# Two-layer hybrid encoder in split single precision: the forms of x for the feed-forward made in the attention's output projection, and pairs 3 to 21 by seven products

## The chip, the cores and the metric

The kernel runs on one core of one Trainium2 chip. The metric is the device time of one launch in microseconds. The core's engines are TensorE (PE: matmuls, with weight loads, PEld, beside them), VectorE (DVE), ScalarE (ACT), GpSimd (POOL, used here almost only to issue accumulating DMAs) and SyncE (SP, which issues the loads).

## What is computed

Two layers over x (512 rows of 1024) with a memory of 256 rows. Each layer has a mixer (attention of two kinds in layer 0, a chunked mLSTM in layer 1), a cross-attention to the memory and a gated feed-forward with a causal convolution of three taps. All in float32.

```python
for layer in range(DEPTH):
    xn = rms_norm(x, mix_norm[layer])
    ...
    x = x + mixed
    x = x + memory_cross_attention(rms_norm(x, xattn_norm[layer]), rms_norm(mem, mem_norm[layer]),
                                   xattn_wq[layer], xattn_wkv[layer], xattn_wo[layer])
    x = x + conv_ffn(rms_norm(x, ffn_norm[layer]), ffn_w_up[layer], ffn_conv_w[layer],
                     ffn_conv_b[layer], ffn_w_down[layer])
return rms_norm(x, final_norm)

def conv_ffn(xn, w_up, conv_w, conv_b, w_down):
    h = causal_depthwise_conv(xn @ w_up, conv_w) + conv_b
    g, u = jnp.split(h, 2, axis=-1)
    return (jax.nn.gelu(g) * u) @ w_down
```

w_up has 1024 x 5632 elements, w_down 2816 x 1024.

## The kernel before

**Numbers.** x lies in SBUF transposed: eight tiles `x[k]` of 128 features by 512 rows. Every float32 operand of a product is cut into two parts that TensorE takes at full rate: hi is a rounded copy (a cast on ACT), lo is the value less hi (`sub`, L265, on DVE; both together are `split`, L267). A product is three matmuls, hi by hi, hi by lo and lo by hi (`mm3`, L271, matmuls on lines 274 to 276). A weight block of 1024 columns comes by SP into one of three `raw` buffers and is split into `wh` and `wl` (three buffers each). So each block costs ACT a cast and DVE a subtraction before PE can use it.

**Cross-attention (`xattn`, L993).** Keys `kth`, `ktl` and values `vh`, `vl` of the memory are split tiles of 128 x 2048 in the stage's pool; the transposed weights of the softmax stand in `pth`, `ptl`; the heads' output rows in `mixed` (heads 0 and 1) and in the buffers `mem` (heads 2 and 3), which held the memory's own rows before. The stage ends with the output projection `p_out` (L375): eight output blocks m, each of eight k, each followed by the sum into x (`xadd`, L492) on DVE and by `xprep` (L478): x times the gain of the next norm on ACT with its split on DVE (`xh`, `xl`), and the sum of squares (`squares`, L461). The blocks run in the order 0 to 7. A planner (`Plan`) orders the tasks of this stage by costs written by hand.

**Feed-forward (`ffn_steps`, L1118).** The up projection has 44 blocks of 128 outputs in 22 pairs: block p (gate) and block 22 + p (value). Each pair ends in `tail` (L1246): convolution (the first tap on ACT, L1256, the other two on DVE, L1263), gelu on ACT, the product (L1273), and a split into `ah`, `al`, ten buffers each. The down projection is cut into five chunks of pairs (`CHUNKS`: four of four pairs, the last of six), each with eight output blocks, whose sums go to x by `xadd`. `fill` (L1424) puts down blocks of a finished chunk between the products of the later pairs from pair 5: three in a seven pair, two in a plain one. The queue gets eight blocks each at pairs 5, 9, 13 and 18; at pair 19 the last four in the queue are held back (`late`) until after pair 21. Then come the eight blocks of the last chunk (in layer 1 in `finish`, with the last norm and the output).

A pair is made in one of two ways.

`plain` (L1290): two blocks of 8 k x 3 matmuls of 512 columns, 48 matmuls, weights loaded by SP into `raw`.

`seven` (L1309): the two weight blocks, halved in the input features, and x, halved in features and in rows, form a 2 x 2 by 2 x 2 product in Winograd's form: seven products of 4 k x 3 matmuls of 256 columns, 84 matmuls. Three of them use x itself (`xh`, `xl`), four use the forms of x, T1 to T4, in `th` and `tl`. The weight side needs sums: `sa` is a load by SP with a second load added to it by POOL's DMA (`onto`, L1317), `sb` is made on DVE (L1340, then L1346), and five splits: f3 and f1 of 1024 columns, `s2`, `s4` and `a22` of 512. The results are put together by five operations of 256 columns on DVE (`sum_`, L1380: `u2`, `u3` and three quarters of `hs`) and two on ACT, and scaled by the norm (`scaled`, L1401). The tiles for `s2`, `s4`, `a22`, `ra`, `v`, `u2` and `u3` have one buffer each, `sb` and `dr` two, `sa` three.

```python
SEVEN = (4, 5, 6, 7, 8, 9, 10, 11, 12, 13, 14, 15, 17, 18, 19, 20)
p6 = pe(n, lambda: opened("Y", by, "acc", s2, 0, *T2, "Y", True), [w2, *formed], [("acc", by)], [("s2", s2)])
p5 = pe(n, lambda: opened("R", br, "s", f1, 512, *T1, "R", True), [w1], [("s", br)])
```

Pairs 0 to 3, 16 and 21 are plain. The forms are made by `forms(k)` (L1222) in the feed-forward, two of the four k after pair 0 and two after pair 1. For k it scales x[k] and x[k + 4] on ACT into an `hs` buffer, makes T1 and T3, T2, T4 on DVE in an `sa` buffer (512, 256 and 256 columns), casts the 1024 columns on ACT and subtracts on DVE. The sum of any down block into x waits on all forms, since they read x.

**Order.** `Sched` in the feed-forward is a list scheduler that runs when the program is built: each task has an engine, a cost and a due time written by hand, and buffers it takes and frees. It fixes the order in which each engine's instructions are issued; on the chip the engines wait on each other by semaphores. SP issues its loads in that order, and a load whose buffer is not free holds up those behind it.

Of the kernel before, what the change touches and what calls it, by code (L numbers as in the profile page):

```python
# [9 lines left out]
F32 = mybir.dt.float32  # L10
# [14 lines left out]

SEVEN = (4, 5, 6, 7, 8, 9, 10, 11, 12, 13, 14, 15, 17, 18, 19, 20)
EPS = 1e-6
# [192 lines left out]
class Builder:  # L220
# [153 lines left out]

    def p_out(self, pl, src, mixed, kdeps, gain, gi, order, prio, reload=False, order0=None):  # L375

        state = {}
        done = []
        for m in range(KB8):
            e = self.p_proj(  # L380
                pl, src[m], mixed, lambda ps, m=m: self.xadd(m, ps, reload), (("D", 0.6),), kdeps=kdeps, order=order, prio=prio + m
            )
            done.append(
                pl.add(lambda m=m: self.xprep(m, gain, gi, state), 0, [e], prio + m, chain=(("A", 0.52), ("D", 0.66), ("A", 0.52)), order=[order0])
            )
        self.state = state
        self.xdone = {k: [d] for k, d in enumerate(done)}

# [336 lines left out]
    def mix0(self):  # L725
        nc, t, tc = self.nc, self.t, self.tc
        with tc.tile_pool(name="mix0", bufs=1, reuse_waits="tile") as mp:
# [61 lines left out]
            def gates(ps):  # L789
                z = rows["z"] = self.til(self.memp, "mem", bufs=8)[:8, :]  # L790
# [135 lines left out]
    def p_memory(self, pl, layer, at, step, order=()):  # L926
# [16 lines left out]
        for k in range(KB8):  # L943

            def prep(k=k):
                both = self.til(mp, "mem", (P, 2, MEM), F32R, bufs=8)
# [46 lines left out]
    def xattn(self, layer):  # L993
        nc, t, tc = self.nc, self.t, self.tc
        with tc.tile_pool(name=f"xa{layer}", bufs=1, reuse_waits="tile") as mp:
            self.mp = mp
            pl = Plan(self.plan, [st["banks"][0] for st in self.fills], s=2, w=2, e=4, q=2, pt=2, wt=3)
            self.pad(mp, 192)
# [3 lines left out]
            vh = mp.tile([P, 2, DM], F32R, name=f"xvh{layer}")  # L1002
            vl = mp.tile([P, 2, DM], F32R, name=f"xvl{layer}")
            norm = self.x_norm(pl, 0, deps=self.xdone[7])
# [3 lines left out]
            for h in range(4):  # L1008
# [48 lines left out]

                def ptget(pts=pts):
                    pts["h"] = self.til(mp, "pth", (P, 2, 512), F32R)
                    pts["l"] = self.til(mp, "ptl", (P, 2, 512), F32R)  # L1060
# [34 lines left out]
                for d in range(2):  # L1095

                    def weigh(h=h, d=d, pts=pts):
# [4 lines left out]
                        b = 2 * h + d  # L1102
                        mh[b], ml[b] = (self.til(mp, "mixed", dtype=F32R, bufs=8) if h < 2 else self.til(self.memp, "mem", dtype=F32R, bufs=8) for _ in range(2))
                        self.split(mh[b][:], ml[b][:], ps[:])
# [13 lines left out]
    def ffn_steps(self, layer, mp):  # L1118
# [22 lines left out]
        RAWS = {"raw": (self.wp, 1024, 3), "dr": (mp, 512, 2), "sa": (mp, 1024, 3), "sb": (mp, 512, 2), "ra": (mp, 512, 1)}  # L1141

        def raw_tile(st, tag):
            pool, n, bufs = RAWS[tag]
            st[tag] = self.til(pool, tag, (P, n), bufs=bufs)
            return st[tag]
# [75 lines left out]
        def forms(k, at):  # L1222

            st = {}

            def scaled(j):
                if j == 0:
                    st["t"] = hs2[st["_hs"]][:, :, 2:514]
                nc.scalar.activation(st["t"][:, j, :512], self.x[k + 4 * j][:], AF.Identity, scale=self.col("ffn", layer * 8 + k + 4 * j))

            def first():
                st["r"] = raw_tile(st, "sa")[:]
                tt_(out=pair(st["r"][:, :512]), in0=pair(st["t"][:, 0, :512]), in1=st["t"][:, :, 256:512], op=ALU.subtract)

            T1, T3, T2, T4 = (slice(256 * i, 256 * i + 256) for i in range(4))
            tt_ = nc.vector.tensor_tensor
            a = add("ACT", ACV, lambda: scaled(0), (), at, [("hs", st)])
            a = add("ACT", ACV, lambda: scaled(1), [a], at)
            a = add("DVE", tt(512), first, [a], at, [("sa", st)])
            a = add("DVE", tt(256), lambda: tt_(out=st["r"][:, T2], in0=st["t"][:, 1, 256:512], in1=st["r"][:, T1], op=ALU.add), [a], at)  # L1240
            a = add("DVE", tt(256), lambda: tt_(out=st["r"][:, T4], in0=st["t"][:, 1, 0:256], in1=st["r"][:, T2], op=ALU.subtract), [a], at, (), [("hs", st)])
            h = add("ACT", act(1024), lambda: nc.scalar.copy(th[k][:], st["r"]), [a], at)
            formed.append(add("DVE", tt(1024), lambda: self.sub(tl[k][:], st["r"], th[k][:]), [h], at, (), [("sa", st)]))


        def tail(p, st, deps, at):  # L1246
# [27 lines left out]

            def hi():
                acts[p] = tuple(self.til(mp, n, dtype=F32R, bufs=10) for n in ("ah", "al"))
                nc.scalar.copy(acts[p][0][:], u())
# [31 lines left out]
        def seven(p, fill):  # L1309
# [16 lines left out]
            def small(s, tag):  # L1326
                if tag == "s4" and not pads:
                    pads.append(self.pad(mp, 64))
                s["wh"], s["wl"] = (self.til(mp, tag + i, (P, 512), F32R, bufs=1) for i in "hl")

# [37 lines left out]
            p1 = pe(n, lambda: opened("X", bx, "acc", f3, 0, *X(0, 0), "X", True), [w3], [("acc", bx)])  # L1368
            p6 = pe(n, lambda: opened("Y", by, "acc", s2, 0, *T2, "Y", True), [w2, *formed], [("acc", by)], [("s2", s2)])
            p5 = pe(n, lambda: opened("R", br, "s", f1, 512, *T1, "R", True), [w1], [("s", br)])  # L1370
            get = rows(st, at + 2.0)

            def v_():
                st["v_"] = self.til(mp, "v", (P, 256), bufs=1)
                nc.scalar.activation(st["v_"][:], st["X"][:, :256], AF.Copy, scale=-1.0)

            def sum_(tag, out, a, b, op):
                if tag:
                    st[tag] = self.til(mp, tag, (P, 256), bufs=1)
                tt_(out=out(), in0=a(), in1=b(), op=op)  # L1380

            bank = lambda n_: (lambda: st[n_][:, :256])
            tmp = lambda n_: (lambda: st[n_][:])
            hs = lambda j, l: (lambda: st["hs_"][:, j, 2 + 256 * l : 258 + 256 * l])
# [26 lines left out]
        def down(c, m, steps=1):  # L1411
# [227 lines left out]
    def finish(self, mp, ah, al):  # L1639
# [6 lines left out]
        HALF = [slice(0, 256), slice(256, 512)]  # L1646
        outs = [self.til(mp, f"t{i}{k}", (P, 1024), F32R, bufs=1).bitcast(F32)[:, s] for k in range(4) for i in "hl" for s in (slice(0, 512),)]

# [19 lines left out]
        def write(ps, t, f, r, vector):  # L1668
            out = outs.pop(0)
            if vector:  # L1670
                nc.vector.tensor_scalar(out=out[:], in0=ps[:], scalar1=r, scalar2=None, op0=ALU.mult)
            else:
                nc.scalar.activation(out[:], ps[:], AF.Identity, scale=r)
            (nc.sync if f else nc.scalar).dma_start(self.t["y"][t][:, f * 512 : f * 512 + 512], out[:])

# [32 lines left out]
    def run(self):  # L1708
        tc = self.tc
        M = bass.MemoryType.PSUM  # L1710
        with (
# [10 lines left out]
            for layer in range(2):  # L1722
                with tc.tile_pool(name=f"mem{layer}", bufs=1, reuse_waits="tile") as self.memp:
                    (self.mix0, self.mix1)[layer]()
                    self.xattn(layer)
                self.ffn(layer)

# [87 lines left out]
```

## Time and profile before

| | us |
|---|---|
| median of 3 runs | 1497.66 (1497.33 to 1498.31) |
| the profiled execution | 1497.39 |
| its span | 1495.6 |
| PE busy in the span | 1483.6 |
| DVE busy | 1194.5 |
| ACT busy | 806.0 |
| feed-forward of layer 0 | about 417 to 758 |
| feed-forward of layer 1, its last part excepted | about 1141 to 1481 |

A row of the timeline gives the start, the duration, engine, line and operation with out<-in. A matmul's duration overlaps with the next one's start, so PE's rate is read from start to start. On DVE too an instruction may start 0.08 us before the one ahead of it has ended by the profile. A row of windows gives for a stretch of time the busy time of each engine and, in brackets, its instructions, then the granted clock, the DMA engines' busy share and GB/s.

### The profile page before, as it was taken

The numbers are of one execution on the slowest core, as the hardware profiler recorded it, in microseconds if no ns is written. First come the engines' busy times: TensorE is split into PE (matmuls) and PEld (weight loads), VectorE is DVE, ScalarE is ACT, GpSimd is POOL, SyncE is SP. The second block draws the span as 40 slices with busy tenths as digits, with TensorE's granted clock in tenths as the row PEclk, the third lists the DMA queues.
The fourth block names the chain that finished last, engine by engine and source line by source line (L and its number), as shares of the span: only waits on it lengthen the run. The fifth ranks groups of instructions, "written<-read, shape, count | busy, mean of one in ns | idle before, by whom it ended". The sixth has DMA issues, their size and how long they took to land.

```text
span 1495.6 us, 22361 instructions
## 1 busy us (share of the span) xinstructions
PE 1483.6 (99%) x8426; PEld 1281.9 (86%) x8426; DVE 1194.5 (80%) x2255; ACT 806.0 (54%) x1349; POOL 57.8 (4%) x100
## 2 busy tenths in 40 slices
PE   9999999999999999999999999999999999999998
PEld 7888777888889999999888778888888899998987
DVE  7779795666589999989768857666567999999974
ACT  7777573444466455555446634444444655555544
POOL 0000130000001000000000000000000000000000
PEclk9999999999999999999999999999999999999999
DMA  5212223323237665542232222323323756564322
GB/s 195 85 63 79 85 86 115 125 74 125 85 127 192 168 157 154 148 120 89 75 99 85 71 99 84 99 93 120 113 72 126 183 156 169 149 162 134 94 65 76
DMA packets 60796, 171.76 MB, mean 115 GB/s; under 512 B 6672, under 2 KB 6672, under 8 KB 60688
## 3 DMA queue, kind: packets, MB, share of 16 engines
q1 hardware_dynamic: 55072, 152.43, 31.2%
q0 software_dynamic: 4608, 16.78, 6.6%
q8 instruction: 66, 1.08, 0.3%
q10 hardware_dynamic: 1008, 1.12, 0.2%
q14 instruction: 42, 0.34, 0.1%
HBM read 168.21 MB, written 2.10 MB: 114 GB/s over the span
## 4 chain that ended last, share of the span: by engine, by line
PE 93%; DVE 4%; ACT 2%; issue 1%; DMA 0%; SPq 0%; DVEq 0%; ACTq 0%
PE acc L274 19%; PE acc L276 19%; PE acc L275 19%; PE w L275 5%; PE w L274 5%; PE w L276 5%; PE s L274 3%; PE acc L335 2%; PE s L276 2%; PE acc L337 2%; PE acc L336 2%; PE s L275 2%; PE w L1603 1%; DVE wl L265 1%; PE s L401 1%
## 5 line engine op out<-in xcount | busy, mean ns | idle before, releaser
L274 PE MATMUL acc<-xh,wh 128*128 128x512 f32 (+1 forms) x832 | 301.3, 362 | 0.0
L276 PE MATMUL acc<-xh,wl 128*128 128x512 f32 (+1 forms) x832 | 296.8, 357 | 0.0
L275 PE MATMUL acc<-xl,wh 128*128 128x512 f32 (+1 forms) x832 | 296.6, 356 | 0.0
L265 DVE TENSOR_TENSOR wl<-raw,wh 128x1024 fp32r<-128x1024 f32 (+2 forms) x201 | 240.5, 1197 | 44.2 <-ACT wh L268 39.9
L268 ACT CAST wh<-raw 128x1024 fp32r<-128x1024 f32 (+2 forms) x137 | 140.6, 1029 | 164.7 <-PE acc L275 97.5
L275 PEld LDWEIGHTS acc<-xl,wh 128*128 128x128 f32 x832 | 157.2, 189 | 22.0
L276 PEld LDWEIGHTS acc<-xh,wl 128*128 128x128 f32 x832 | 156.2, 188 | 22.7
L274 PEld LDWEIGHTS acc<-xh,wh 128*128 128x128 f32 x832 | 156.3, 188 | 22.1
L1263 DVE SCALAR_TENSOR_TENSOR c<-hs,vec,c 128x512 f32<-128x512 f32 x176 | 128.8, 746 | 4.5 <-ACT c L1256 3.7
L275 PE MATMUL w<-al,wh 128*128 128x512 f32 x304 | 118.6, 390 | 0.0
L274 PE MATMUL w<-ah,wh 128*128 128x512 f32 x304 | 118.5, 390 | 0.0
L276 PE MATMUL w<-ah,wl 128*128 128x512 f32 x304 | 118.4, 389 | 0.0
L1256 ACT ACTIVATE c<-hs,vec 128x512 f32<-128x512 f32 x88 | 69.8, 813 | 52.9 <-DVE hs L1401 46.5
L276 PEld LDWEIGHTS w<-ah,wl 128*128 128x128 f32 x304 | 57.0, 188 | 12.0
L274 PEld LDWEIGHTS w<-ah,wh 128*128 128x128 f32 x304 | 57.1, 188 | 10.2
L275 PEld LDWEIGHTS w<-al,wh 128*128 128x128 f32 x304 | 57.1, 188 | 10.1
L495 DVE TENSOR_TENSOR x<-w,x 128x512 f32<-128x512 f32 x72 | 49.3, 685 | 16.1 <-PE w L276 16.1
L274 PE MATMUL acc<-mem,wh 128*128 128x256 f32 (+1 forms) x192 | 61.5, 320 | 0.0
L276 PE MATMUL acc<-mem,wl 128*128 128x256 f32 (+1 forms) x192 | 61.0, 318 | 0.0
L275 PE MATMUL acc<-mem,wh 128*128 128x256 f32 (+1 forms) x192 | 60.8, 317 | 0.0
L495 DVE TENSOR_TENSOR x<-acc,x 128x512 f32<-128x512 f32 x32 | 22.1, 690 | 46.6 <-PE acc L276 46.6
L1165 ACT CAST wh<-dr 128x512 fp32r<-128x512 f32 x64 | 39.5, 617 | 35.7 <-PE w L275 18.4
(373 smaller groups left out, 3798.2 us busy)
## 6 DMA issues: line engine op xcount, KB each, us to landing
raw<-in_up_dram SPq DMA_DIRECT2D x56, 512.0 KB, 3.3
dr<-in_down_dram SPq DMA_DIRECT2D x64, 256.0 KB, 2.9
sa<-in_up_dram SPq DMA_DIRECT2D x32, 512.0 KB, 3.5
sa<-in_up_dram POOLq DMA_DIRECT2D x32, 512.0 KB, 5.6
raw<-in_xk_dram SPq DMA_DIRECT2D x16, 512.0 KB, 3.2
raw<-in_wo_dram SPq DMA_DIRECT2D x16, 512.0 KB, 3.3
raw<-in_xq_dram SPq DMA_DIRECT2D x16, 512.0 KB, 3.2
raw<-in_xv_dram SPq DMA_DIRECT2D x16, 512.0 KB, 3.2
```

Of the source, the lines that this page charges most:

```text
L265: self.nc.vector.tensor_tensor(out=lo, in0=v, in1=hi.bitcast(F32), op=ALU.subtract)
L268: self.nc.scalar.copy(hi, v)
L274: mm(out, wh, xh, start=first, stop=False, skip_group_check=parts)
L275: mm(out, wh, xl, start=False, stop=False, skip_group_check=parts)
L276: mm(out, wl, xh, start=False, stop=last, skip_group_check=parts)
L335: mm(ps, xh[k][:, ts], wh[:, ws], start=(k == 0), stop=False)
L336: mm(ps, xh[k][:, ts], wl[:, ws], start=False, stop=False)
L337: mm(ps, xl[k][:, ts], wh[:, ws], start=False, stop=(k == 7))
L495: self.nc.vector.tensor_tensor(out=self.x[m][:], in0=ps[:], in1=self.x[m][:], op=ALU.add)
L1165: nc.scalar.copy(st["wh"][:, :cols], st[tag][:, :cols])
L1256: nc.scalar.activation(st["c_"][:, j, :], hs()[:, j, 2:514], AF.Identity, scale=self.col("cw", (layer * 3 + 2) * 44 + blk), bias=self.col( ...
L1263: nc.vector.scalar_tensor_tensor(out=c, in0=hs()[:, j, n : n + 512], scalar=w, in1=c, op0=ALU.mult, op1=ALU.add)
```

## The change

1. `SEVEN` becomes 3 to 21: pairs 3, 16 and 21 of each layer are made by seven products too. Six pairs more in all.
2. `forms` leaves the feed-forward. `p_forms` makes the same four groups in the output projection. The projection's blocks run in the order 0, 4, 1, 5, 2, 6, 3, 7, so that x[k] and x[k + 4] follow each other, and the forms of k come after block k + 4. Their scratch lies in the buffers `pth` and `ptl`.
3. The keys and values get tiles of their own, `kv0` to `kv3` (128 x 2048 each), in a pool that lives through cross-attention and feed-forward. `th` and `tl` are written into them when the attention is done with them; the feed-forward's own tiles for `th` and `tl` are gone.
4. Small tiles of the feed-forward move into buffers that lie idle there: `s2h`, `s2l`, `a22h`, `a22l`, `ra`, both `dr` and one `sb` into `mem0` to `mem7`; `v` into `memrb`, `u2` and `u3` into the two buffers of `sqt`. The number of buffers of each stays. `finish` writes its outputs from `kv0` and `kv1`.
5. At pair 19 the last six down blocks of the queue are held back. Five are left in the queue then, so all of them run after pair 21.
6. The tasks that waited on `formed` no longer do. Two tasks without instructions (4.0 on DVE, 3.0 on ACT) stand at the head of the feed-forward's plan.

```diff
-SEVEN = (4, 5, 6, 7, 8, 9, 10, 11, 12, 13, 14, 15, 17, 18, 19, 20)
+SEVEN = (3, 4, 5, 6, 7, 8, 9, 10, 11, 12, 13, 14, 15, 16, 17, 18, 19, 20, 21)
...
-    def p_out(self, pl, src, mixed, kdeps, gain, gi, order, prio, reload=False, order0=None):
+    def p_out(self, pl, src, mixed, kdeps, gain, gi, order, prio, reload=False, order0=None, ms=range(KB8), after=None):
...
+            if after and m >= 4:
+                after(m - 4, done[m] + done[m - 4], prio + n)
...
+    def p_forms(self, pl, layer, k, deps, prio):
...
+        th, tl = self.form(0, k), self.form(1, k)
...
+        def one():
+            g = st["g"] = self.til(self.mp, "pth", (P, 2, 512), F32)
+            r = st["r"] = self.til(self.mp, "ptl", (P, 2, 512), F32)[:].rearrange("p a b -> p (a b)")
+            for j in range(2):
+                nc.scalar.activation(g[:, j, :], self.x[k + 4 * j][:], AF.Identity, scale=self.col("ffn", layer * 8 + k + 4 * j))
+            tt(out=r[:, :512].rearrange("p (a b) -> p a b", a=2), in0=g[:, 0, :].rearrange("p (a b) -> p a b", a=2), in1=g[:, :, 256:512], op=ALU.subtract)
+            tt(out=r[:, T2], in0=g[:, 1, 256:512], in1=r[:, T1], op=ALU.add)
+            tt(out=r[:, T4], in0=g[:, 1, 0:256], in1=r[:, T2], op=ALU.subtract)
+
+        def two():
+            nc.scalar.copy(th, st["r"])
+            self.sub(tl, st["r"], th)
+
+        a = pl.add(one, 0, deps, prio, chain=(("A", 1.04), ("D", 1.28)))
+        pl.add(two, 0, [a], prio, chain=(("A", 0.95), ("D", 1.14)))
+
+    def form(self, i, k):
+        return self.kv[2 * i + k // 2][:, k % 2 * 1024 : k % 2 * 1024 + 1024]
...
-            kth = mp.tile([P, KB8, MEM], F32R, name=f"kth{layer}")
-            ktl = mp.tile([P, KB8, MEM], F32R, name=f"ktl{layer}")
+            kth, ktl = (a[:].rearrange("p (a b) -> p a b", a=KB8) for a in self.kv[:2])
+            vh, vl = (a[:].rearrange("p (a b) -> p a b", a=2) for a in self.kv[2:])
...
-            self.p_out(pl, t["xo"][layer], lambda: (mh, ml), kd, "ffn", layer, None, 100)
+            self.p_out(pl, t["xo"][layer], lambda: (mh, ml), kd, "ffn", layer, None, 100, ms=(0, 4, 1, 5, 2, 6, 3, 7), after=lambda *a: self.p_forms(pl, layer, *a))
...
+        for n, (tag, i) in enumerate([("s2h", 0), ("s2l", 0), ("a22h", 0), ("a22l", 0), ("ra", 0), ("dr", 0), ("dr", 1), ("sb", 1)]):
+            HOMES[tag, i] = f"mem{n}"
...
-        th, tl = ([mp.tile([P, 1024], F32R, name=f"t{i}{layer}{k}", tag=f"t{i}{k}") for k in range(4)] for i in "hl")
-        formed, pads = [], []
+        th, tl = ([self.form(i, k) for k in range(4)] for i in range(2))
+        pads = []
...
+        add("DVE", 4.0, None, (), -20.0)
+        add("ACT", 3.0, None, (), -20.0)
...
-            p6 = pe(n, lambda: opened("Y", by, "acc", s2, 0, *T2, "Y", True), [w2, *formed], [("acc", by)], [("s2", s2)])
+            p6 = pe(n, lambda: opened("Y", by, "acc", s2, 0, *T2, "Y", True), [w2], [("acc", by)], [("s2", s2)])
...
-            e = add("DVE", 0.6, lambda: self.xadd(m, d["ps"]), [last, xadded[m], *formed], clock[0] + 3.0, (), [("w", d)])
+            e = add("DVE", 0.6, lambda: self.xadd(m, d["ps"]), [last, xadded[m]], clock[0] + 3.0, (), [("w", d)])
...
-                queue, late = queue[:-4], queue[-4:]
+                queue, late = queue[:-6], queue[-6:]
             (seven if p in SEVEN else plain)(p, fill if p >= 5 else lambda: None)
-            if p < 2:
-                for k in (2 * p, 2 * p + 1):
-                    forms(k, clock[0] + 4.0 * (k % 2))
```

More of the change, by code (lines that the diff above doesn't have):

```diff
@@ L373, in xs @@
         return self.xh, self.xl
-    def p_out(self, pl, src, mixed, kdeps, gain, gi, order, prio, reload=False, order0=None):
+    def p_out(self, pl, src, mixed, kdeps, gain, gi, order, prio, reload=False, order0=None, ms=range(KB8), after=None):
         state = {}
-        done = []
-        for m in range(KB8):
+        done = {}
+        for n, m in enumerate(ms):
             e = self.p_proj(
-                pl, src[m], mixed, lambda ps, m=m: self.xadd(m, ps, reload), (("D", 0.6),), kdeps=kdeps, order=order, prio=prio + m
+                pl, src[m], mixed, lambda ps, m=m: self.xadd(m, ps, reload), (("D", 0.6),), kdeps=kdeps, order=order, prio=prio + n
@@ L382, in p_out @@
             )
-            done.append(
-                pl.add(lambda m=m: self.xprep(m, gain, gi, state), 0, [e], prio + m, chain=(("A", 0.52), ("D", 0.66), ("A", 0.52)), order=[order0])
-            )
+            done[m] = [pl.add(lambda m=m: self.xprep(m, gain, gi, state), 0, [e], prio + n, chain=(("A", 0.52), ("D", 0.66), ("A", 0.52)), order=[order0])]
+            if after and m >= 4:
+                after(m - 4, done[m] + done[m - 4], prio + n)
         self.state = state
-        self.xdone = {k: [d] for k, d in enumerate(done)}
+        self.xdone = done
@@ new lines, in p_forms @@
+    def p_forms(self, pl, layer, k, deps, prio):
+        nc = self.nc
+        tt = nc.vector.tensor_tensor
+        T1, T3, T2, T4 = (slice(256 * i, 256 * i + 256) for i in range(4))
+        th, tl = self.form(0, k), self.form(1, k)
+        st = {}
+        def one():
[11 more added lines that the diff above has]
+        pl.add(two, 0, [a], prio, chain=(("A", 0.95), ("D", 1.14)))
@@ L789, in gates @@
             def gates(ps):
-                z = rows["z"] = self.til(self.memp, "mem", bufs=8)[:8, :]
+                z = rows["z"] = self.til(self.memp, "mem0", bufs=1)[:8, :]
                 self.gate_rows(z, ps, 0, 32, 8, "foxb")
@@ L945, in prep @@
             def prep(k=k):
-                both = self.til(mp, "mem", (P, 2, MEM), F32R, bufs=8)
+                both = self.til(mp, f"mem{k}", (P, 2, MEM), F32R, bufs=1)
                 self.mem.append((both[:, 0, :], both[:, 1, :]))
@@ L1102, in weigh @@
                         b = 2 * h + d
-                        mh[b], ml[b] = (self.til(mp, "mixed", dtype=F32R, bufs=8) if h < 2 else self.til(self.memp, "mem", dtype=F32R, bufs=8) for _ in range(2))
+                        if b == 0:
+                            self.pad(mp, 64)
+                        mh[b], ml[b] = (
+                            self.til(mp, "mixed", dtype=F32R, bufs=8) if h < 2 else self.til(self.memp, f"mem{2 * b - 8 + i}", dtype=F32R, bufs=1) for i in range(2)
+                        )
                         self.split(mh[b][:], ml[b][:], ps[:])
@@ L1220, in ffn_steps @@
             nc.gpsimd.memset(h[:, :, 0:2], 0.0)
[L1222 to L1243, printed above, removed]
+        add("DVE", 4.0, None, (), -20.0)
+        add("ACT", 3.0, None, (), -20.0)
         def tail(p, st, deps, at):
@@ L1646, in finish @@
         HALF = [slice(0, 256), slice(256, 512)]
-        outs = [self.til(mp, f"t{i}{k}", (P, 1024), F32R, bufs=1).bitcast(F32)[:, s] for k in range(4) for i in "hl" for s in (slice(0, 512),)]
+        outs = [kv[:, 512 * i : 512 * i + 512] for kv in (self.til(self.kvp, f"kv{i}", (P, 2048), bufs=1) for i in range(2)) for i in range(4)]
         def add(m, ps, c):
@@ L1724, in run @@
                     (self.mix0, self.mix1)[layer]()
-                    self.xattn(layer)
-                self.ffn(layer)
+                    with tc.tile_pool(name=f"kv{layer}", bufs=1, reuse_waits="tile") as self.kvp:
+                        self.pad(self.kvp, 192)
+                        self.kv = [self.til(self.kvp, f"kv{i}", (P, 2048), F32R, bufs=1) for i in range(4)]
+                        self.xattn(layer)
+                        self.ffn(layer)
 def col_blocks(w):
```

30 lines of the change are left out of this document (19 added, 11 removed).

## The prediction

> **What bounds the kernel now.** I read the head of the profile's page first, then the PE rows of a pair of each kind, then the windows of each stage, and last the groups and the timeline of DVE in the feed-forward.
>
> ```profile
> span 1495.6 us, 22361 instructions
> PE 1483.6 (99%) x8426; PEld 1281.9 (86%) x8426; DVE 1194.5 (80%) x2255; ACT 806.0 (54%) x1349; POOL 57.8 (4%) x100
> PEclk9999999999999999999999999999999999999999
> PE 93%; DVE 4%; ACT 2%; issue 1%; DMA 0%; SPq 0%; DVEq 0%; ACTq 0%
> ```
>
> PE is busy 99% of the span, at the full granted clock, and is 93% of the chain of waits. So an edit is worth what it takes from PE, less what it makes PE wait. The profiled execution took 1497.39 us, 1.8 more than its span and 0.27 under the median of the three runs (1497.66); the sum below starts at 1497.39.
>
> ```profile
> core 0: us, PE busy (x) PEld busy (x) DVE busy (x) ACT busy (x) POOL busy (x), PEclk, DMA share, GB/s
> 410.00:420.00 10.00, 10.00 (x46) 8.28 (x45) 6.03 (x8) 5.46 (x8) 0.00 (x0) 1.00 0.48 167
> 450.00:460.00 10.00, 10.00 (x46) 8.28 (x45) 10.00 (x16) 6.06 (x8) 0.97 (x2) 1.00 0.96 243
> 507.85:523.06 15.21, 15.21 (x110) 14.25 (x109) 14.62 (x23) 6.87 (x11) 0.84 (x1) 1.00 0.64 173
> 645.42:656.30 10.88, 10.88 (x49) 9.01 (x48) 9.84 (x14) 5.62 (x8) 0.00 (x0) 1.00 0.29 97
> 656.30:709.61 53.31, 53.27 (x398) 50.47 (x396) 49.26 (x77) 28.75 (x45) 0.87 (x1) 1.00 0.33 91
> 418.00:758.20 340.20, 340.07 (x2153) 307.30 (x2152) 312.25 (x491) 185.26 (x279) 14.38 (x18) 1.00 0.49 135
> ```
>
> The first of these windows is the output projection of the first layer, the last its whole feed-forward; between them lie the first pairs, pair 7 with two down blocks, pair 16 (plain), and pairs 17 to 20. Two things are to be seen. PE has no gap in the feed-forward (340.07 of 340.20). But DVE stands right behind it there: 312 of 340 on the mean, and 10.00 of 10.00 at 450 to 460, where PE is at 10.00 too. In the output projection DVE has 4 us in 10 free.
>
> **The gain: what PE is given.** A plain pair has 48 matmuls of 512 columns; one by seven products has 84 of 256.
>
> ```profile
> 507.85 0.28 PE L274 MATMUL acc<-xh,wh 128*128 128x256 f32 x1
> ...
> 509.26 0.29 PE L274 MATMUL acc<-th,s2h 128*128 128x256 f32 x1
> ...
> 510.64 0.28 PE L274 MATMUL s<-th,wh 128*128 128x256 f32 x1
> ```
>
> Pair 16 runs from 645.42 to 656.30 in the windows above: 10.88 us, or 0.2267 for a matmul. A down block of 12 such is 2.72. Pair 7 runs 15.21 with two down blocks in it: 15.21 - 5.44 = 9.77. Its products one by one: 12 matmuls with xh and xl take 509.26 - 507.85 = 1.41, 12 with the forms (th, tl) 510.64 - 509.26 = 1.38; three of the first kind and four of the second make 9.75. I take 9.75. The change turns pairs 3, 16 and 21 of each layer from plain to seven: 6 x (10.88 - 9.75) = 6.8 us less on PE. [...] All other products stay as many. A loss in rate isn't excluded for the products with forms, because th and tl now lie in other tiles; that is rival C.
>
> **The cost: what DVE is given.** The durations by form, and the starts of one stretch in which DVE never waits:
>
> ```profile
> L1263 DVE SCALAR_TENSOR_TENSOR c<-hs,vec,c 128x512 f32<-128x512 f32 x88 | 64.4, 746 | 2.2 <-ACT c L1256 1.8
> L265 DVE TENSOR_TENSOR wl<-raw,wh 128x1024 fp32r<-128x1024 f32 x26 | 31.7, 1220 | 1.5 <-ACT wh L1334 0.9 <-ACT wh L1165 0.4
> L265 DVE TENSOR_TENSOR wl<-dr,wh 128x512 fp32r<-128x512 f32 x32 | 21.9, 684 | 0.0
> L1380 DVE TENSOR_TENSOR u<-acc,v 128x256 f32<-128x256 f32 x32 | 13.4, 418 | 0.5 <-PE acc L276 0.4
> L265 DVE TENSOR_TENSOR tl<-sa,th 128x1024 fp32r<-128x1024 f32 x4 | 4.9, 1222 | 0.0
> ```
> ```profile
> 470.05 1.22 DVE L265 TENSOR_TENSOR wl<-sa,wh 128x1024 fp32r<-128x1024 f32 x1
> 471.18 0.42 DVE L1380 TENSOR_TENSOR u<-acc,v 128x256 f32<-128x256 f32 x1
> 471.51 0.68 DVE L1273 TENSOR_TENSOR c<-c 128x512 f32<-128x512 f32 x1
> 472.11 0.41 DVE L1380 TENSOR_TENSOR hs<-u,s 128x256 f32<-128x256 f32 x1
> ```
>
> Back to back each costs 0.08 less than its duration: 1.14 (1024 wide), 0.60 (512), 0.34 (256), 0.66 (a tap of the convolution). A seven pair has 3, 7, 5 and 4 of them: 3.42 + 4.20 + 1.70 + 2.64 = 11.96. A plain pair has 2, 4, 0 and 4: 7.32. So each of the six pairs gives DVE 4.64 more while PE has 1.13 less to cover it. Without down blocks a seven pair leaves DVE behind PE by 11.96 - 9.75 = 2.2; a down block (0.60 + 0.60 on DVE, 2.72 on PE) gives back 1.5, so three in a pair more than make it up.
>
> The forms leave the feed-forward: per group 0.60 + 2 x 0.34 + 1.14 = 2.42 of DVE, four groups, 9.7 a layer. Against 3 x 4.64 = 13.9 a layer, DVE's load in the feed-forward rises by only 4.2, and PE's falls by 3.4. On the mean 316 of 337 us still fits. So it is a question of places.
>
> *The output projection.* The four groups now run after blocks 4, 5, 6 and 7, one for every two blocks.
>
> ```profile
> 400.65 0.69 DVE L495 TENSOR_TENSOR x<-acc,x 128x512 f32<-128x512 f32 x1 [2.04 <-PE acc L276]
> ...
> 406.09 0.69 DVE L495 TENSOR_TENSOR x<-acc,x 128x512 f32<-128x512 f32 x1 [2.09 <-PE acc L276]
> ```
> ```profile
> 405.86 1.05 ACT L1165 CAST wh<-raw 128x1024 fp32r<-128x1024 f32 x1 [3.24 <-PE acc L275]
> 406.82 0.72 ACT L475 ACTIVATE xh<-x,vec 128x512 fp32r<-128x512 f32 x1
> 407.44 0.62 ACT L469 ACTIVATE sqt<-x 128x512 f32<-128x512 f32 x1
> ```
>
> A block lasts 406.09 - 400.65 = 5.44 on PE, and DVE waits 2.09 of it, ACT 3.24. Two blocks have 4.2 of DVE and 6.5 of ACT free; a group asks 2.42 of DVE and, by these rows, 2 x 0.62 + 0.96 = 2.2 of ACT. The projection's weights are a block ahead, so a split that stands behind a group comes no later than PE asks for it: 0 us on PE. Without that cover a group's 2.42 would stand between a block's split and PE. The last group, which cannot start before the last block, falls into plain pair 0, whose products need no forms, and pair 3 is 32.6 us away; before the change the first group ran at the same place, beside the sums of the norm. I take 0, with 0.5 a layer as the upper end.
>
> ```profile
> 414.06 0.38 SPq L1151 DMA_DIRECT2D ra<-in_up_dram  x1
> 414.50 0.90 SPq L1151 DMA_DIRECT2D dr<-in_down_dram  x2
> ```
>
> On SP's queue these first loads of ra and dr go into tiles of the memory's keys now, which the projection reads to its end, 406.09 + 2 x 5.44 = 417.0: 2.5 to 2.9 us later than before. Behind them on the queue stand the loads of pair 2 and of pair 3's sums, the nearest of which PE asks for 20 us later: 0.
>
> *Pairs 3 to 9.* Pairs 0 to 2 are plain and free of forms now: DVE is 3 x (10.88 - 7.32) = 10.7 ahead in work, where weight buffers let it, before pairs 3 and 4 take 2 x 2.2. From pair 5 to 6 the down blocks give it back. Pair 3's loads (512 KB by SP, 512 KB added by POOL, then 512 and 256 KB by SP) come at the feed-forward's start.
>
> ```profile
> sa<-in_up_dram SPq DMA_DIRECT2D x32, 512.0 KB, 3.5
> sa<-in_up_dram POOLq DMA_DIRECT2D x32, 512.0 KB, 5.6
> ra<-in_up_dram SPq DMA_DIRECT2D x32, 256.0 KB, 2.9
> L1340 DVE TENSOR_TENSOR sb<-sa,raw 128x512 f32<-128x512 f32 x16 | 10.9, 686 | 1.1 <-DMA raw<-in_up_dram 1.0
> ```
>
> A converted pair moves 1.79 MB in place of 1.05. Load and addition land 3.5 + 5.6 = 9.1 us after the first issue, and pair 3 has three plain pairs of time; the forms no longer hold the sa buffers there. The busiest window (450 to 460, DMA share 0.96) is where SP's queue is fullest; DVE's whole wait for DMA at L1340 is 1.0 us in 16 pairs, so six more cost 0 to 0.4 together; I take 0. [...]
>
> *Pairs 16 to 21.* Here is the cost. The down blocks of the last full chunk run in pairs 18 (three) and after 21 (five); pairs 16, 17, 19, 20 and 21 have none. In the order in which the changed kernel issues, between the last product of pair 16 and the product of pair 21 with s4, PE has 375 matmuls of 256 columns and 50 of 512: 375 / 84 x 9.75 + 50 x 0.2267 = 43.5 + 11.3 = 54.8. DVE has in between 12, 34, 24 and 19 instructions of the four kinds: 13.7 + 20.4 + 8.2 + 12.5 = 54.8. They are level, with DVE's lead at the end of pair 16 as the only cushion; before, the window of pairs 17 to 20 showed 49.26 less 77 x 0.08 = 43.1 of 53.31. Whatever DVE then waits for ACT, PE or DMA lands on PE once the lead is used. Over the whole feed-forward those waits are the last columns of the groups above, 0 to 2 us a row; in the window 450 to 460 they are 0. Lower bound: the lead (up to 5 us from pairs 13 to 15: 3 x 9.75 + 8 x 2.72 = 51.0 of PE against 45.5 of DVE) covers all, 0. Upper bound: two of the five uncovered pairs show in full, 4.4. I take 0.5 a layer, near the lower, as DVE enters with a lead and the waits of a full DVE are near 0.
>
> After pair 21 its tail (taps, gelu, split) must end before the last chunk's first block asks for pair 21's rows; five down blocks, 13.6 us, stand in between, against a chain of some 9.5 (scaling 1.2, two conv passes with taps 4.3, product 0.7, cast 0.6, split 0.7, and two down blocks' DVE work between, 2.0): 0.
>
> Small tiles in other buffers, the dummy tasks of the planner and the dropped waits on the forms issue nothing: 0.
>
> Sum: 1497.4 - 6.8 + 2 x 0.5 = 1491.6; bounds 1490.6 (no stall) and 1497.4 - 6.8 + 2 x (0.5 + 4.4) = 1500.4.
>
> **Rivals.**
> A. *DVE sets the pace from pair 16 on, in part.* For it: the level sum, 54.8 to 54.8, and windows with DVE at 10.00. Against: the lead from pairs 13 to 15. One uncovered pair a layer, and its waits: 1.25 to 2.5 each, 1493.1 to 1495.6; I put it at 1494.
> B. *Slower.* The lead doesn't survive, as a seven's single s2, s4 and a22 buffers keep DVE from working more than a pair ahead: each of the five pairs without downs then costs PE its 2.2. At most 11 a layer, and 1497.4 - 6.8 + 22 = 1512.6. It decides from 3.4 a layer, one and a half such pairs: above that the gain is gone. Against: before the change pairs 4, 8 and 12 stood without downs, and PE had 340.07 of 340.20.
> C. *The change does not deliver: the products with forms run no faster than those with x.* The forms' 1.38 against 1.41 goes with where th lies. If it goes, 4 x 0.03 x 19 x 2 = 4.6 us are lost over both layers: 1491.6 + 4.6 = 1496.2, about no change. [...]
>
> **How the numbers follow.** Forecast 0.68, A 0.17, B 0.06, C 0.05, the rest (0.04) below the forecast, with products a little faster than the rows of pair 7. The forecast has its own range 1490.3 to 1493.0; with A the range is 1490.0 to 1495.0. This kernel's runs lie within 0.07%, and I count less than 0.2% (3.0 us) as no change: faster is below 1494.7, slower above 1500.7. Faster: forecast, the rest, and most of A, 0.88; same: the end of A, C and a part of B, 0.07; slower 0.05.
>
> **What would show it.** Right: PE busy 6.8 lower, the plain-to-seven pairs at 9.75, PE idle in the feed-forward under 1 us a layer, no PE gap in the output projection, and the rows of tl at 1.22 there. DVE near 10.00 in every window from pair 16 to pair 21. Wrong: PE waits ended by DVE (c22, u2 or a split before s4) in pairs 16 to 21 above 1 us a layer (A, B), products with forms at 1.41 (C), or waits for DMA at the sums of pair 3.

## The result and the profile after

The changed kernel takes 1503.53 us (median of 6 runs, 1501.91 to 1504.05), the kernel before 1497.58 on the same chip: a ratio of 1.0036, 95% interval 1.0025 to 1.0047. It is slower by some 6 us, where 1491.6 was forecast with a range of 1490.3 to 1493.0.

The head of the page of the changed kernel:

```profile
span 1502.2 us, 22929 instructions
PE 1483.3 (99%) x8642; PEld 1288.1 (86%) x8642; DVE 1219.6 (81%) x2309; ACT 820.6 (55%) x1379; POOL 63.9 (4%) x106
PE 82%; DVE 10%; DMA 3%; issue 2%; ACT 2%; SPq 0%; DVEq 0%; ACTq 0%; POOLq 0%
```

PE's share of the chain fell from 93% to 82%, DVE's rose from 4% to 10%, and DMA, which was at 0%, is at 3%. PE's matmuls for the norm stand at both ends of a feed-forward, so their starts measure it. First the kernel before, then the changed one (timeline, layer 0):

```profile
420.48 0.27 PE L1200 MATMUL s<-ones,sq 128*128 128x2 f32 x1
...
767.73 0.50 PE L401 MATMUL s<-ones,sq 128*128 128x2 f32 x4
```
```profile
420.95 0.36 PE L1243 MATMUL s<-ones,sq 128*128 128x2 f32 x2
...
770.57 0.28 PE L429 MATMUL s<-ones,sq 128*128 128x2 f32 x2
```

347.25 us before, 349.62 after. With three pairs at 1.13 less it should have been 343.9, so 5.8 us are lost in this layer. The windows say where (the columns are those of the windows in the prediction). First one of the kernel before, then the changed one:

```profile
426.00:441.00 15.00, 15.00 (x68) 12.25 (x67) 12.25 (x24) 9.81 (x13) 0.00 (x0) 1.00 0.26 84
```
```profile
426.00:441.00 15.00, 15.00 (x67) 12.24 (x67) 9.01 (x18) 6.44 (x8) 2.72 (x3) 1.00 1.01 270
...
456.00:459.00 3.00, 0.37 (x3) 0.37 (x4) 2.96 (x5) 2.33 (x5) 0.86 (x1) 1.00 0.22 81
459.00:463.00 4.00, 4.00 (x24) 3.96 (x23) 3.83 (x7) 1.48 (x3) 0.00 (x0) 0.58 0.83 136
...
660.00:680.00 20.00, 19.98 (x158) 18.98 (x156) 19.90 (x33) 12.03 (x21) 1.70 (x2) 1.00 0.67 168
680.00:700.00 20.00, 19.86 (x150) 19.00 (x151) 20.00 (x33) 11.99 (x18) 0.00 (x0) 1.00 0.27 79
700.00:720.00 20.00, 19.88 (x156) 18.78 (x155) 19.82 (x33) 11.28 (x19) 0.00 (x0) 1.00 0.21 61
```

From 426 to 441 the DMA engines are full (1.01, where they were at 0.26) and DVE works only 9.0 of 15 us, where it worked 12.25. PE feels nothing of it yet. From 456 to 459, in pair 3, PE stands still, and in the 4 us after that its granted clock is 0.58. In pairs 16 to 21 (660 to 720), where the forecast looked for the cost, DVE is full as expected, and PE's gaps come to 0.28 us.

The steps between are in the timelines of the queues and engines. SP, POOL, then DVE, ACT and PE of the changed kernel (start, duration; in brackets the idle time before and what ended it):

```profile
416.99 0.42 SPq L1194 DMA_DIRECT2D mem<-in_up_dram  x1
...
419.63 0.33 SPq L1194 DMA_DIRECT2D raw<-in_up_dram  x1
423.69 0.33 SPq L1194 DMA_DIRECT2D mem<-in_up_dram  x1
424.07 1.46 SPq L1194 DMA_DIRECT2D sa<-in_up_dram  x3
```
```profile
429.20 1.01 POOL L1342 DMA_DIRECT2D sa<-in_up_dram  x1 [54.71 <-DMA sa<-in_up_dram]
431.86 0.86 POOL L1342 DMA_DIRECT2D sa<-in_up_dram  x1 [1.65 <-DMA sa<-in_up_dram]
```
```profile
422.98 0.68 DVE L265 TENSOR_TENSOR mem<-mem,mem 128x512 fp32r<-128x512 f32 x1
...
438.13 0.69 DVE L1364 TENSOR_TENSOR sb<-sa,raw 128x512 f32<-128x512 f32 x1 [2.93 <-DMA sa<-in_up_dram]
...
441.68 0.69 DVE L1364 TENSOR_TENSOR mem<-sa,raw 128x512 f32<-128x512 f32 x1 [2.25 <-DMA sa<-in_up_dram]
```
```profile
457.50 0.81 ACT L1278 ACTIVATE c<-hs,vec 128x512 f32<-128x512 f32 x1
458.22 0.36 ACT L1399 ACTIVATE memrb<-acc 128x256 f32<-128x256 f32 x1
```
```profile
455.60 0.28 PE L276 MATMUL s<-kv,wl 128*128 128x256 f32 x1
458.63 0.39 PE L274 MATMUL acc<-xh,wh 128*128 128x256 f32 x1 [2.76 <-ACT memrb L1399]
```

Read from the top. The load of ra for pair 3 (`mem`, from up) leaves SP at 416.99. ra has one buffer, and its next load, for pair 4, comes at 423.69: it waited until DVE had split pair 3's a22 (422.98 + 0.68 = 423.66). The three loads of the sums stand behind it and leave at 424.07. Three at once with the weights, they keep the first addition, that of pair 3, waiting till 429.20 (5.1 us; the median before was 3.5), and its landing ends DVE's wait at 438.13 (8.9 us after its issue; 5.6 before). In DVE's order the sum of pair 3 stands at 435.2, after the taps of pair 0, and DVE waits there with all that is behind it, 2.93 us, and for pair 4's sum another 2.25. With two pairs without down blocks ahead DVE does not get this time back. ACT's queue runs late with DVE's taps: v (`memrb`) is made at 458.22 behind a convolution, and the second x product of pair 3 waits for v: 2.76 us of PE. Layer 1 has the same wait at 1183.55, of 2.25 us.

### The profile page after: what moved, and what is told of

The parts are those of the page before. It is cut to its first block, busy times and chain, and to the rows that moved or that the text cites. A ratio compares the mean times of both kernels' runs of the same rounds, so it can differ in the third digit from the quotient of the medians.

```text
span 1502.2 us, 22929 instructions
## 1 busy us (share of the span) xinstructions
PE 1483.3 (99%) x8642; PEld 1288.1 (86%) x8642; DVE 1219.6 (81%) x2309; ACT 820.6 (55%) x1379; POOL 63.9 (4%) x106
## 4 chain that ended last, share of the span: by engine, by line
PE 82%; DVE 10%; DMA 3%; issue 2%; ACT 2%; SPq 0%; DVEq 0%; ACTq 0%; POOLq 0%
PE acc L274 16%; PE acc L276 16%; PE acc L275 16%; PE w L276 5%; PE w L275 5%; PE w L274 5%; PE acc L335 2%; PE acc L337 2%; PE acc L336 2%; PE s L274 2%; PE s L276 2%; DVE wl L265 2%; PE s L275 2%; DVE c L1285 2%; PE w L1624 1%
## 5 line engine op out<-in xcount | busy, mean ns | idle before, releaser
L274 PE MATMUL acc<-xh,wh 128*128 128x512 f32 (+1 forms) x784 | 278.2, 355 | 5.0 <-ACT memrb L1399 5.0
L276 PE MATMUL acc<-xh,wl 128*128 128x512 f32 (+1 forms) x784 | 273.7, 349 | 0.0
L275 PE MATMUL acc<-xl,wh 128*128 128x512 f32 (+1 forms) x784 | 273.2, 349 | 0.0
L265 DVE TENSOR_TENSOR wl<-raw,wh 128x1024 fp32r<-128x1024 f32 (+2 forms) x195 | 233.0, 1195 | 42.6 <-ACT wh L268 39.7
L274 PEld LDWEIGHTS acc<-xh,wh 128*128 128x128 f32 x784 | 148.0, 189 | 24.1 <-ACT memrb L1399 5.4
L275 PEld LDWEIGHTS acc<-xl,wh 128*128 128x128 f32 x784 | 149.0, 190 | 18.6
L276 PEld LDWEIGHTS acc<-xh,wl 128*128 128x128 f32 x784 | 147.9, 189 | 19.1
L274 PE MATMUL acc<-kv,mem 128*128 128x256 f32 x304 | 84.6, 279 | 0.0
L275 PE MATMUL acc<-kv,mem 128*128 128x256 f32 x304 | 84.4, 278 | 0.0
L276 PE MATMUL acc<-kv,mem 128*128 128x256 f32 x304 | 84.3, 277 | 0.0
L1208 ACT CAST wh<-mem 128x512 fp32r<-128x512 f32 x64 | 39.6, 619 | 42.4 <-PE acc L275 17.4
L274 PE MATMUL acc<-mem,wh 128*128 128x256 f32 (+1 forms) x192 | 61.5, 321 | 0.0
```

The lines of the kernel that those rows point to most:

```text
L265: self.nc.vector.tensor_tensor(out=lo, in0=v, in1=hi.bitcast(F32), op=ALU.subtract)
L274: mm(out, wh, xh, start=first, stop=False, skip_group_check=parts)
L275: mm(out, wh, xl, start=False, stop=False, skip_group_check=parts)
L276: mm(out, wl, xh, start=False, stop=last, skip_group_check=parts)
L1208: nc.scalar.copy(st["wh"][:, :cols], st[tag][:, :cols])
```

## The experiments

All ratios are to the kernel before, measured beside each on the same chip. The first five groups start from the changed kernel.

**Fewer bytes in the additions**, every engine's order unchanged. The additions of pairs 3 to 5 leave out three quarters of their columns, so the sums of these pairs lack that part.

```diff
-b1 = onto(lambda: sa["sa"][:], lambda: A2, 1024, [b1], at - 16.0)
+nc_ = 256 if p in (3, 4, 5) else 1024
+b1 = onto(lambda: sa["sa"][:, :nc_], lambda: A2[:, :nc_], 1024, [b1], at - 16.0)
```

> The changed kernel with the additions by POOL's DMA cut to a quarter (256 of 1024 columns) for pairs 3, 4 and 5 alone; the weight sums of these pairs miss the rest of their second term. The order of every engine's instructions is the same. Theory DMA (the loads and additions of pairs 3 to 5, all between 424 and 441 us, share one bandwidth; pair 3's and 4's sums land late, DVE loses 5.2 us at 435 to 441, and PE 2.8 us at 456 and a slower clock after it): DVE's waits of 2.9 and 2.3 us for sa vanish, PE's wait of 2.8 and 2.3 us before pair 3's second x product vanish, and so does the clock of 0.50: 2 x 5.1 us less, some 1493 us. Theory load (pair 3 simply gives DVE more than it can do before PE asks, with or without the waits for DMA): PE's wait stays above 2 us a layer and the time above 1501.

1497.25 us (1495.44 to 1498.56), 0.9996 (0.9987 to 1.0006), against 1503.53; some 1493 was expected. DVE and windows of its profiled execution (1495.44 us):

```profile
435.17 0.68 DVE L1365 TENSOR_TENSOR sb<-sa,raw 128x512 f32<-128x512 f32 x1
...
437.49 0.69 DVE L1365 TENSOR_TENSOR mem<-sa,raw 128x512 f32<-128x512 f32 x1 [1.03 <-DMA raw<-in_up_dram]
```
```profile
426.00:441.00 15.00, 15.00 (x68) 12.21 (x67) 12.48 (x23) 7.07 (x9) 2.71 (x3) 1.00 0.68 198
```

The DMA share falls from 1.01 to 0.68, DVE's waits for sa are gone, and so is PE's at 456; DVE's wait of 1.0 us for weights is left, and one of 0.6 us of PE before the product with s4. The instructions are the same, so the load on DVE alone does not make the stall. The median is 1.8 us above the profiled execution; what the other runs waited for is open.

**ra and the first sb changed over**, which takes ra's loads out of the sums' way on SP's queue.

```diff
-("ra", 0), ("dr", 0), ("dr", 1), ("sb", 1)
+("sb", 0), ("dr", 0), ("dr", 1), ("sb", 1)
```

> The changed kernel with two tiles changed over: ra in the feed-forward's own pool, the first sb in the memory's buffer in its place. So SP's queue has the loads of the sums of pairs 3 and 4 ahead of ra's loads, and no wait of ra for the split of a22 (422.98) stands before them; the same loads, the same bytes. Theory queue (the sums' loads were issued at 424.1 because ra's second load held the queue, and bandwidth then did the rest): the loads start at about 420, the additions of pairs 3 and 4 land some 4 us earlier, DVE waits for them 0 to 2 us in place of 5.2, PE 0 to 1 us in place of 2.8, the clock stays at 1.00: 1493 to 1497. Theory bandwidth alone (the landing is set by the bytes asked for, not by the place in the queue): landing within 1.5 us of the changed kernel's, time 1501 or more.

1495.05 us (1494.07 to 1496.17), 0.9983 (0.9974 to 0.9993): 8.5 us less than the changed kernel, and faster than before. SP, POOL and DVE:

```profile
419.47 0.95 SPq L1194 DMA_DIRECT2D sa<-in_up_dram  x2
420.46 0.47 SPq L1194 DMA_DIRECT2D ra<-in_up_dram  x1
```
```profile
424.46 1.01 POOL L1342 DMA_DIRECT2D sa<-in_up_dram  x1 [50.50 <-DMA sa<-in_up_dram]
```
```profile
434.76 0.68 DVE L1364 TENSOR_TENSOR mem<-sa,raw 128x512 f32<-128x512 f32 x1
...
439.51 0.68 DVE L1364 TENSOR_TENSOR mem<-sa,raw 128x512 f32<-128x512 f32 x1
```
```profile
426.00:441.00 15.00, 15.00 (x67) 12.12 (x66) 13.58 (x24) 9.56 (x13) 1.71 (x2) 1.00 0.98 248
```

The sums' loads leave 4.6 us sooner, the addition starts at 424.46 in place of 429.20, and DVE makes both sums with no wait. The DMA engines are about as full as in the changed kernel (0.98 from 426 to 441, 1.01 there), so with the same bytes an earlier start is enough. Both count, then: with fewer bytes a late start costs little, with an early start the bytes cost nothing that DVE waits for.

**ra alone moved**, 2 KB a partition more, sb where the change put it. This parts ra's place from sb's.

```diff
-("ra", 0), ("dr", 0), ("dr", 1), ("sb", 1)
+("x", 0), ("dr", 0), ("dr", 1), ("sb", 1)
```

> The changed kernel with one tile moved: ra in the feed-forward's own pool (2 KB a partition more), sb where the change put it. Theory queue (ra's loads ahead of the sums' loads on SP's queue are what makes the sums late): the sums' loads start at about 420, DVE waits for sa 0 to 1 us, PE has no wait above 0.5 us at 456 to 466; the same time as with ra and sb changed over, 1494.3 to 1496.0. Theory other place (it was sb's place that helped there): above 1500.

1495.06 us (1494.61 to 1495.90), 0.9981 (0.9972 to 0.9990): the same.

```profile
419.83 0.95 SPq L1194 DMA_DIRECT2D sa<-in_up_dram  x2
420.82 0.47 SPq L1194 DMA_DIRECT2D ra<-in_up_dram  x1
```

It is ra's place that counts, and with it the place of its loads on the queue. The order on DVE changes too: the split of pair 3's a22 starts at 433.50 and 433.87 in these two kernels, not at 422.98. That gives DVE one split more just ahead of the sum, not one less, so it is not what helps. How the place of a tile comes to change the order on the engines is not shown.

**Pair 3 plain again** (`SEVEN` from 4 to 21), and, beside it, **the forms moved and nothing else** (pairs of before), and **pair 3 alone** by seven with the forms moved.

> The changed kernel with pair 3 plain again; pairs 16 and 21 stay by seven products, the forms stay in the output projection. Theory early (the whole miss is pair 3's): no wait of PE at 456, no fall of the clock; 1503.5 - 2 x 5.1 + 2 x 1.13 = 1495.6, and PE's gaps in pairs 16 to 21 stay at about 1.1 us a layer. Theory late (the pairs from 16 on without down blocks cost as much): 1500 or more.

> The changed kernel with the pairs of before (3, 16 and 21 plain) and the last four down blocks held back as before: the forms made in the output projection, the tiles in their new places, nothing else. Theory free move (the forms fit into DVE's and ACT's idle time there, and their going from pairs 0 and 1 frees work that PE did not wait for): within 1 us of the kernel before, 1496.7 to 1498.2. Theory costly move (a part of the miss is the move itself, by weights that come late in the projection or by the sums' loads): 1499 or more.

> The kernel with the forms moved and of the three pairs pair 3 alone by seven products (16 and 21 plain, four down blocks held back). Theory early (pair 3's sums are late, and this is the whole miss): PE's wait of 2.3 to 2.8 us before pair 3's second x product and the granted clock of 0.50 after it are there as in the changed kernel; 1497.6 - 2.3 + 10.3 = 1505.6. Theory together (pair 3 is late only because pairs 4 to 21 leave DVE no time): below 1499.

1495.05 (0.9982, 0.9973 to 0.9992), 1497.57 (0.9999, 0.9989 to 1.0008) and 1504.86 (1.0046, 1.0031 to 1.0061). Moving the forms costs nothing and gives nothing (there the sums' loads leave as late, at 423.54, but they are for pair 4 on). Pair 3 alone costs 7.3 us against that, though it takes 2.3 from PE: 9.6 us of stall, 4.8 a layer. The rest of the change, pairs 16 and 21, brings 2.5.

**PE kept at work in its wait.**

```diff
+            if p == 3:
+                def warm():
+                    for i in range(24):
+                        nc.tensor.matmul(st["R"][:, 256:512], f1["wh"][:, 512:640], th[0][:, 0:256], start=True, stop=True, skip_group_check=True)
+                pe(0.0, warm, [p5], (), ())
```

> The changed kernel with 24 matmuls of 256 columns more in pair 3 of each layer, into an unused half of the bank s, between its third product and the one that waits for v. They fill PE's wait (24 x 0.115 = 2.75 us) with work that nothing uses; the wait itself stays, as v comes no sooner. Theory clock (the fall of the granted clock to 0.50 for some 3.4 us is PE's answer to the idle time, and costs 1.5 us a layer): the granted clock stays at 1.00 from 456 to 464, the product after the wait starts at the same time as before, and the time falls by 3 us to about 1500.5. Theory no matter (the fall has another cause, or DVE sets the pace there anyway): within 0.7 us of 1503.5.

1502.05 us (1501.51 to 1503.60), 1.5 less than the changed kernel where 3 was expected. The ranges of the two overlap, and so do the intervals of their ratios (1.0018 to 1.0042 against 1.0025 to 1.0047), so the time alone decides little. (These matmuls write into the other half of R's bank, and pair 3's results are not those of the changed kernel; the other instructions are the same.) Its window, the next wait, and the same wait in the kernel with pair 3 alone:

```profile
456.00:464.00 8.00, 7.81 (x68) 7.61 (x66) 7.62 (x12) 4.97 (x9) 0.86 (x1) 1.00 0.61 132
```
```profile
465.17 0.38 PE L274 MATMUL s<-xh,s4h 128*128 128x256 f32 x1 [1.36 <-DVE hs L1404]
```
```profile
457.71 0.38 PE L274 MATMUL acc<-xh,wh 128*128 128x256 f32 x1 [2.52 <-ACT memrb L1399]
...
465.37 0.38 PE L274 MATMUL s<-xh,s4h 128*128 128x256 f32 x1 [1.42 <-DVE hs L1404]
```

The clock stays at 1.00, as the clock theory says, but four products later PE waits 1.36 us for DVE, where the changed kernel waited 0.19. With pair 3 alone the clock did not fall in spite of 2.52 us of idle time, and there too PE waits 1.42 at that place. By these rows the slow clock mostly took the place of a wait: DVE sets the pace through the whole pair.

**Pairs 16 to 21**, from the kernel with ra and sb changed over: pair 16 plain; four, and then three, down blocks held back in place of five.

```diff
-queue, late = queue[:-6], queue[-6:]
+queue, late = queue[:-4], queue[-4:]
```

> The kernel with ra and the first sb changed over, and pair 16 plain again (PE 1.13 a layer more, DVE 4.6 less ahead of pairs 17 to 21). Theory level (what pair 16 saves PE, DVE takes back in the pairs after it): PE's gaps in pairs 16 to 21 fall by 0.6 to 1.1 us a layer, and the time stays within 1 us: 1495.0 to 1496.1. Theory gain (pair 16's saving is real): gaps as they are, 1497.3.

> The kernel with ra and the first sb changed over, and the last four down blocks held back in place of five, so that one of them stands in pair 19. Theory level (in pairs 16 to 21 DVE and PE are level, and a down block there leaves DVE 1.5 us): PE's gaps there fall from about 1.1 to 0.3 to 0.8 us a layer: 1493.7 to 1494.8. Theory tail (four down blocks, 10.9 us, no longer cover pair 21's tail of some 9.5 with its waits): a wait of PE for al before the last chunk, 1496 or more.

> The same with three down blocks held back, 8.2 us of PE between the end of pair 21 and the last chunk. Theory tail (the chain of taps, gelu and split after pair 21 takes some 9.5 us): PE waits 1 to 3 us a layer for al before the last chunk's first block, 1496 to 1499. Theory slack (the chain is shorter, or its pieces come earlier): 1493 to 1494.5, as one more down block relieves DVE in pairs 19 to 21.

1495.22 (0.9981, 0.9972 to 0.9991), 1493.99 (0.9974, 0.9964 to 0.9983) and 1494.33 (0.9979, 0.9970 to 0.9988). With pair 16 plain the time is the same and DVE has room: two of its windows, beside 19.90 and 19.82 of the changed kernel:

```profile
660.00:680.00 20.00, 20.00 (x149) 18.87 (x148) 18.60 (x32) 10.79 (x17) 0.86 (x1) 1.00 0.64 158
...
700.00:720.00 20.00, 20.00 (x146) 18.85 (x145) 18.56 (x33) 10.68 (x18) 0.53 (x1) 1.00 0.20 53
```

PE is busy 20.00 of 20 in both, and 19.86 and 19.87 with pair 16 by seven. For pair 16 theory level holds. For the down block in pair 19 it is open: 1493.99 lies in its range, but the same kernel gave 1494.93 below, beside 1495.05 without that block. Theory tail falls: three blocks, 8.2 us, still cover the tail of pair 21, as PE waits only 0.2 us for `ah` in that kernel; the chain of 9.5 was put too long, or parts of it are done sooner.

**Four down blocks held back, with pair 3 by seven and plain**, side by side.

> The kernel with ra and sb changed over and four down blocks held back, once more beside the one with pair 3 plain: 1494.0 within 0.7 us by all theories.

> The kernel with ra and sb changed over and four down blocks held back, with pair 3 plain. Theory full DVE (between 430 and 480 us DVE has no idle time left once pair 3 is seven, so what pair 3 saves PE, 1.13 a layer, comes back as PE's gaps at 461 and 481): no difference to the same kernel with pair 3 by seven, within 0.8 us of 1494.0. Theory gain (with the sums in time pair 3 pays in full): 1496.2.

1494.93 (0.9981, 0.9972 to 0.9990) and 1494.78 us (0.9980, 0.9971 to 0.9989). With its sums in time pair 3 costs nothing, and it pays nothing either. The first is the kernel that gave 1493.99 on another chip. The kernels with ra out of the sums' way lie within 1.3 us of each other (1493.99 to 1495.22), and which of them is best cannot be said. All are faster than the kernel before and the changed one.

## Why the prediction was wrong

**What bounds the kernel.** Right: PE up to the point where DVE has no time left.

**The gain, 6.8 us.** Right in size, as far as the products go. In the kernel with ra and sb changed over, pair 7's take 1.41 us with x (507.27 to 508.68) and 1.38 with forms (508.68 to 510.06), as before. The kernel with the forms alone moved has 16 pairs a layer with four products each out of the new tiles, and takes no longer than before, so rival C (0.03 a product, 3.8 us there) falls. The feed-forward of the kernel with ra and sb changed over shows what is left of the gain (layer 0):

```profile
420.41 0.25 PE L1243 MATMUL s<-ones,sq 128*128 128x2 f32 x1
...
765.71 0.39 PE L429 MATMUL s<-ones,sq 128*128 128x2 f32 x3
```

345.30, or 1.95 less than before, of the 3.4 that three pairs take from PE.

**The forms in the output projection, 0.** Right: the kernel with the forms alone moved is level with the one before.

**SP's queue and pairs 3 to 9, both put at 0: the steps that failed.** Three errors stand in them.
1. "2.5 to 2.9 us later than before" looked at the first loads of ra and dr only. Behind them on the queue is ra's second load, which waits for the split of the first: the sums left at 424.07, not at the 419.47 of the kernel with ra and sb changed over. The profile before had this wait already, DVE's row ending at 423.21 and SP's following it; there no sum stood behind it:

```profile
422.53 0.68 DVE L265 TENSOR_TENSOR a22l<-ra,a22h 128x512 fp32r<-128x512 f32 x1
```
```profile
423.24 0.33 SPq L1151 DMA_DIRECT2D ra<-in_up_dram  x1
```

2. "3.5 + 5.6 = 9.1 us" added the medians of all such transfers in a feed-forward where the DMA share is 0.49 on the mean. Three loads, three additions and the weights fall together here at a share of 1.01, and it was 5.1 + 8.9 = 14.0. With a quarter of the additions' bytes DVE's wait for them was gone; by what an addition with all its bytes takes 8.9 us in place of 5.6 is not shown.
3. "The nearest of which PE asks for 20 us later" measured the slack to PE. But the sum is an instruction on DVE, in a fixed place at 435.2, and all of DVE's later work stands behind it. 435.2 - 424.07 leaves 11.1 us for 14.0.

The price that was bounded at 0 to 0.4 us for six pairs measured 4.8 a layer, with pair 3 alone. The prediction named the sign of it ("waits for DMA at the sums of pair 3") but gave it no rival and no price; rival B, the slower one, sat in pairs 16 to 21.

**Pairs 16 to 21, 0.5 a layer.** The mechanism was right (level, shown by pair 16 plain), the size was half of what was measured. With pair 3 plain the time fell by 1497.6 - 1495.05 = 2.5 where two pairs a layer take 4.5: 1.0 a layer is given back. In the windows of the changed kernel (layer 0) only 0.28 of it shows as gaps. Rival A's price of 1.25 to 2.5 begins above that.

**What was missed in the rest.** With ra and sb changed over the kernel is at 1495.05 and not at 1491.6: some 1.0 a layer in pairs 16 to 21 where 0.5 stood, and pair 3's 1.13 a layer given back in full. That it is given back is shown by the kernels with pair 3 plain; where is only in part seen. With ra and sb changed over DVE has 18.5, 19.2 and 20.0 us of work in the three windows of 20 from 440 to 500, and PE's gaps there come to 0.25 us. That makes 1491.6 + 1.0 + 2.3 = 1494.9.

## What to carry to other kernels

When loads are moved to the start of a stage, walk each queue entry by entry and ask of each what it waits for: one load whose single buffer is freed by the stage's own work holds up everything behind it (here the sums' loads left at 424.07 in place of 419.47). Measure a load's slack to the instruction that reads it, on an engine that works in order, not to the engine that sets the pace (11.1 us here, where 20 were counted); and time transfers by how many run at once, not by their medians (14.0 us here at a DMA share of 1.01, 9.1 by the medians). Where two engines are level, taking work from one pays only until the other is full, and a pair given to it past that point pays nothing (1494.93 us with pair 3 by seven, 1494.78 with it plain).

## What the runs showed of the hardware

The granted clock of the changed kernel fell to 0.50 twice before its last matmul: at 459.68, 1.05 us after the end of a wait of PE of 2.76 us (455.88 to 458.63), and in layer 1 at 1183.30, 0.25 us before the end of one of 2.25 (1181.30 to 1183.55). It stayed there for 3.41 us each time. Windows within the two stretches, then the matmuls of 256 columns, which start every 0.213 us there:

```profile
459.69:463.08 3.39, 3.39 (x18) 3.35 (x17) 3.18 (x6) 1.47 (x2) 0.00 (x0) 0.50 0.74 141
1183.31:1186.70 3.39, 3.15 (x14) 3.15 (x15) 3.35 (x7) 0.87 (x3) 0.26 (x1) 0.50 0.72 118
```
```profile
462.52 0.41 PE L274 MATMUL acc<-kv,wh 128*128 128x256 f32 x1
462.73 0.41 PE L275 MATMUL acc<-kv,wh 128*128 128x256 f32 x1
462.94 0.36 PE L276 MATMUL acc<-kv,wl 128*128 128x256 f32 x1
463.14 0.28 PE L274 MATMUL acc<-xh,wh 128*128 128x256 f32 x1
463.26 0.28 PE L275 MATMUL acc<-xl,wh 128*128 128x256 f32 x1
```

At 1.00, where the last two of these rows stand, they start 0.12 us apart; in pair 7 of the kernel before it was 0.115 to 0.118 on the mean of a product, and in its pair 16, with 512 columns, 0.227.

In the kernel with pair 3 alone PE was idle for 2.52 us (455.20 to 457.71), and the clock stayed at 1.00:

```profile
455.00:458.00 3.00, 0.48 (x4) 0.29 (x3) 2.96 (x5) 2.33 (x5) 0.86 (x1) 1.00 0.22 84
458.00:460.00 2.00, 1.85 (x16) 1.65 (x16) 1.96 (x5) 0.17 (x1) 0.00 (x0) 1.00 0.73 100
460.00:463.00 3.00, 3.00 (x29) 3.00 (x27) 2.66 (x5) 2.31 (x4) 0.00 (x0) 1.00 0.81 153
463.00:466.00 3.00, 1.58 (x14) 1.38 (x13) 2.96 (x6) 1.10 (x2) 0.00 (x0) 1.00 0.68 257
```

It stayed there too with PE's wait filled by matmuls (1.00 from 456 to 464). The length of the wait alone does not account for the falls: the clock fell with one of 2.25 us and not with one of 2.52. What else decides is not shown.
